# The openings of two feed-forward blocks: a tile in another ring, one split later, and another order ahead of the fourth token tile

## The chip, the cores and the metric

The kernel runs on one core of one Trainium2 chip. The core has five engines that work side by side, each through a queue of its own in order: TensorE (PE, matrix products), VectorE (DVE), ScalarE (ACT), GpSimd (POOL) and SyncE (SP), which here issues the transfers (DMA). They wait for each other by semaphores. The metric is the device time of one execution in microseconds (us). Before the change it is 2113.74 us, the median of 3 runs (2113.13 to 2113.86).

## The reference

One layer of a decoder trunk for 1024 tokens of width 1024, in float32: a feed-forward block, two attention branches with gates, and a second feed-forward block. Only the feed-forward blocks matter here:

```python
def rms_norm(x, gain):
    y = xf * lax.rsqrt(jnp.mean(xf * xf, axis=-1, keepdims=True) + RMS_EPS)
    return y * gain
def swiglu(x, w_gate, w_up, w_down):
    return (jax.nn.silu(x @ w_gate) * (x @ w_up)) @ w_down
...
x = x + 0.5 * swiglu(rms_norm(x, ffn1_norm), ffn1_w_gate, ffn1_w_up, ffn1_w_down)
x = x + mixer(x)
x = x + 0.5 * swiglu(rms_norm(x, ffn2_norm), ffn2_w_gate, ffn2_w_up, ffn2_w_down)
```

The hidden width is 2816, which is 22 tiles of 128.

## The kernel before

**Numbers.** Each float32 operand of a product is split into two float16 parts, a high one (a cast on ACT) and a low one (the remainder, on DVE); a product is then three matmuls (`mm3`): high by high, high by low, low by high. `part` runs one of these three for a whole tile and calls them H (weight high, tokens high), M (weight high, tokens low) and L (weight low, tokens high). Weights are first scaled by a power of two that comes from a bound on their size: `plain` holds the steps for a weight pair that is used as it is, `sums` (absolute sums, ACT), `spread` (two small matmuls into `mx`, a reduction and some one-column steps on DVE), `hi` (ACT) and `lo` (DVE).

**The opening of FFN 1** (`start`). The 1024 tokens lie in 8 token tiles of 128. `norm_steps` gives each tile six steps by letter: q square and row sum (ACT) and the reciprocal root (one step on ACT, three on POOL for tiles 1 to 7), s the product with root and gain into a buffer `y` of the ring (DVE), t eight transposes into a bank pair `psa` (PE), h high part (ACT), r a raw copy for the tiles 4 to 7 (ACT), l low part (DVE). `go` runs such steps in the order of its arguments. The first pair of weight tiles (gate and up, `p0`) is multiplied with tokens 0 to 511 (tiles 0 to 3) while tiles 4 to 7 are being prepared: H for gate and up, then M, M, L, L with a token tile's transposes between them.

**The rest of the opening** (`ffn_up`). The other half of the tokens for pair 0 (its result `a0` is written to DRAM), then pair 1 (`p1`) in full through `proj_T` (products `p2` and `p3`, result `a`). Pairs 2 to 21 are done in `hidden_tile` with seven products of sums in place of eight (Strassen's scheme): steps 0 to 6, each of 12 matmuls with an operand `op` made of weights (`split`, a cast on ACT at L164 and a low part on DVE at L165) and one made of tokens (`token_sums`: `total`, `high`, `low` for the four sums t1 to t4). Step 6 of a tile is put behind step 0 of the next one (`finish`). Step 6 reuses the bank `a` after DVE's L922 has read it. For tile 2 the sum t4 (`total(4)`, `high(4)`, `low(4)`) is made during the tile, through the list `mid`: it is the token operand of step 6.

**Rings.** `self.ring.tile` with a tag takes one of `bufs` buffers (two for each tag here); the next user of a buffer waits until its last use is over, and a transfer to DRAM counts as a use. The ring `y` holds the `y` of the token tiles, both halves `a0` of pair 0, `a` of pair 1 and the `sums` of the weight pairs (POOL). The ring `atp` holds the gain, the two halves of t3 and every fourth `op`; the other ops go to `stg`, `whi`, `wlo`.

**Order.** Inside `with self.in_order(...)` ACT, DVE and PE keep the order of the code; elsewhere (tiles 3 to 21, POOL, SP) a scheduler sets the order. FFN 2 runs the same `ffn_up`, but its tiles 4 to 7 are prepared in `first_half`.

Of the kernel before, what the change touches and what calls it, by code (L numbers as in the profile page):

```python
# [9 lines left out]
F32 = mybir.dt.float32  # L10
F32R = mybir.dt.float32r
BF16 = mybir.dt.bfloat16
F16 = mybir.dt.float16
I32 = mybir.dt.int32
AF = mybir.ActivationFunctionType
ALU = mybir.AluOpType
AX = mybir.AxisListType

P = 128
# [3 lines left out]
KD = D // P  # L23
# [13 lines left out]
HALF = 512  # L37
# [27 lines left out]
class Layer:  # L65
# [132 lines left out]
    def plain(self, loads, norm, engine=None):  # L198

        nc = self.nc  # L200
        st = self.sm.tile([P, 6], F32, tag="bst", bufs=2, name="bst")
        flat = lambda w: w.rearrange("p k n -> p (k n)")
        box = {}

        def sums():
            last = self.latest(mybir.EngineType.Activation)
            for k, w in enumerate(loads):
                nc.scalar.activation(
                    self.spare[:, :512].bitcast(BF16), flat(w), AF.Abs, accum_out=st[:, k:k + 1]
                )  # L210
                self.follow(last)

        def biggest():
            for k, w in enumerate(loads):
                nc.vector.tensor_reduce(
                    out=st[:, k:k + 1], in_=flat(w), op=ALU.max, axis=AX.X, apply_absolute_value=True
                )

        def spread():
            m = st[:, 5:6]  # L220
            self.spread_max(st, len(loads), m)
            box["s"], box["inv"] = self.pow2(m, 14, st[:, 2:5], norm["inv"])

        def hi():
            h, l = (self.ring.tile([P, 2, KD, P], F16, tag=t, bufs=2, name=t) for t in ("whi", "wlo"))
            box["w"] = [(h[:, a], l[:, a]) for a in range(2)]
            for (o, _), w in zip(box["w"], loads):
                nc.scalar.activation(o, w, AF.Copy, scale=box["s"])

        def lo():  # L230
            for (h, o), w in zip(box["w"], loads):
                nc.vector.scalar_tensor_tensor(
                    out=flat(o), in0=flat(w), scalar=box["s"], in1=flat(h), op0=ALU.mult, op1=ALU.subtract
                )

        box.update(sums=sums, biggest=biggest, spread=spread, hi=hi, lo=lo)
        return box

# [95 lines left out]
    def start(self, norm, loads, small, row, tags):  # L334
        ET = mybir.EngineType
        nc = self.nc
        steps = lambda t: self.norm_steps(norm, t, nc.gpsimd if t else None)
        with self.in_order(ET.Activation, ET.DVE, ET.PE):
# [21 lines left out]
            n = {t: steps(t) for t in range(4)}  # L360
            p0 = self.plain([l[0] for l in loads], norm, nc.gpsimd)
            go = lambda *a: [n[int(b[1])][b[0]]() for b in a]
# [1 line left out]
            self.scale_gain(norm)  # L364
            go("t0", "q1", "h0", "s1", "t1", "q2", "l0", "q3", "h1", "s2", "t2")
            p0["sums"]()
            go("l1", "s3", "t3", "h2")
            p0["spread"]()
            n.update({t: steps(t) for t in range(4, NT)})
            ahead = {j: self.pair_load("ffn1", j, tags["w"]) for j in (2, 3)}  # L370
            go("l2", "h3")
            p0["hi"]()
            go("q4", "l3")
            banks = pg, pu = self.psbg(), self.psbg()
            (wg, wu), (hi, lo) = p0["w"], (norm[k][0] for k in ("hi", "lo"))
            self.part(pg, wg, hi, lo, "H")
            self.part(pu, wu, hi, lo, "H")
            p0["lo"]()
            p1 = self.plain([l[0] for l in self.ffn_loads("ffn1", 1)], norm, nc.gpsimd)
            go("q5", "s4", "t4")  # L380
            self.part(pg, wg, hi, lo, "M")
            go("h4", "r4", "s5", "t5", "l4", "q6")
            self.part(pu, wu, hi, lo, "M")
            go("h5", "r5", "s6", "l5", "q7", "t6")
            self.part(pg, wg, hi, lo, "L")
            go("s7", "h6", "r6", "l6", "t7")
            self.part(pu, wu, hi, lo, "L")
            go("h7", "r7", "l7")
            self.mark()
# [268 lines left out]
    def ffn_up(self, norm, name, p0, p1, banks, tags, loads, ready):  # L658
# [5 lines left out]
        nc = self.nc  # L664
# [3 lines left out]
        total, high, low, every = self.token_sums(norm)  # L668
# [6 lines left out]

        def out(n, pg, pu):
            s = slice(n * HALF, (n + 1) * HALF)
            a = self.ring.tile([P, HALF], F32, tag="y", bufs=2, name="a0")
            nc.scalar.activation(a, pg, AF.Silu, scale=p0["inv"])
            nc.vector.scalar_tensor_tensor(out=a, in0=pu, scalar=p0["inv"], in1=a, op0=ALU.mult, op1=ALU.mult)  # L680
            nc.sync.dma_start(dst[0][:, s], a)

        with self.in_order(ET.Activation, ET.DVE, ET.PE):
# [33 lines left out]
            ops = [next(nxt) for _ in range(2)]  # L717
# [3 lines left out]
            a = self.ring.tile([P, T], F32, tag="y", bufs=2, name="a")  # L721
# [4 lines left out]
            nc.vector.scalar_tensor_tensor(out=a, in0=p3, scalar=p1["inv"], in1=a, op0=ALU.mult, op1=ALU.mult)  # L726
            nc.sync.dma_start(dst[1], a)
            tile = self.up_tiles(norm, name, tags, loads, stats, scales, sumd)
            ops, finish = tile(2, ops, every, None, (lambda: total(4), lambda: (high(4), low(4))))
        for j in range(3, NH):  # L730
            ops, finish = tile(j, ops, every, finish, ())
        finish()
# [148 lines left out]
    def hidden_tile(self, ops, tok, e, nxt, finish, then, inv, late, mid):  # L881


        nc = self.nc
# [8 lines left out]
        def prep():  # L893
            new.extend(o for o in (next(nxt, None),) if o is not None)
# [21 lines left out]
        step(4, c, False)  # L916
        v(out=e[:, 1], in0=c, in1=e[:, 1], op=ALU.add)
        nc.scalar.activation(e[:, 1], e[:, 1], AF.Silu, scale=inv)
        prep()
        step(5, a, False)  # L920
        stt = nc.vector.scalar_tensor_tensor
# [942 lines left out]
```

## Time and profile before

| what | before |
|---|---|
| median of 3 runs | 2113.74 us |
| the profiled execution | 2112.18 us |
| its span (first to last instruction) | 2110.4 us |
| mean granted TensorE clock | 0.994 |
| PE / DVE / ACT / POOL busy | 98% / 63% / 50% / 33% |

The times in the views are microseconds from the start of the span. The duration of a row of matmuls is modelled and overlaps the next one a little. "Granted clock" is the share of its full clock at which PE was allowed to run. In names, an arrow points from what is read to what is written: `psa<-ident,y` are transposes of a `y` into `psa`. A group `x8` is eight like instructions in one row.

### The profile page before, as it was taken

What the parts mean: (1) busy time and instruction counts of PE and PEld (TensorE: products, weight loads), DVE (VectorE), ACT (ScalarE), POOL (GpSimd) and SP (SyncE); (2) the same over time, 40 slices, a digit from 0 to 9 for tenths busy, and PEclk for the clock granted to TensorE, in tenths of its full rate; (3) what the DMA queues carried; (4) which work ended last, traced back from release to release, by engine and by line L of the source; (5) the groups of instructions that cost most, each with busy time, mean ns of one, the idle gap of its engine ahead of it and who ended that gap; (6) DMA issues with size and microseconds to landing.
All of it is one profiled execution on the core that took longest, in us unless ns stands there. A gap on an engine that the chain in (4) does not pass through costs nothing.

```text
span 2110.4 us, 28351 instructions
## 1 busy us (share of the span) xinstructions
PE 2077.0 (98%) x10199; PEld 1436.4 (68%) x10199; DVE 1330.4 (63%) x2317; ACT 1054.6 (50%) x1845; POOL 697.1 (33%) x741
## 2 busy tenths in 40 slices
PE   7999999999999999999999999999999999999999
PEld 4444444458888888888888888888444444448887
DVE  6755555577776787455656677864754545559765
ACT  7555555534444554356656775422555555544442
POOL 2355554572301112123333432000244555465200
PEclk8999999999999999999999999999999999999999
DMA  7134243464424387664556683641443433355432
GB/s 205 55 101 149 87 139 100 140 255 158 131 91 161 109 229 203 219 168 138 142 140 153 183 221 114 219 140 66 107 128 100 139 100 119 121 190 214 135 101 109
DMA packets 251638, 304.87 MB, mean 144 GB/s; under 512 B 17785, under 2 KB 186601, under 8 KB 251498
## 3 DMA queue, kind: packets, MB, share of 16 engines
q1 hardware_dynamic: 251498, 303.07, 47.2%
q8 instruction: 80, 1.31, 0.3%
q14 instruction: 60, 0.49, 0.1%
HBM read 205.02 MB, written 98.00 MB: 144 GB/s over the span
## 4 chain that ended last, share of the span: by engine, by line
PE 86%; DVE 5%; ACT 3%; DMA 3%; issue 2%; POOL 1%; SPq 0%; ACTq 0%; POOLq 0%; DVEq 0%
PE pst L876 18%; PE psd L1026 17%; PE psb L876 10%; PE pss L1647 4%; PE psg L876 3%; PE pspt L1673 3%; PE psgate L154 3%; PE psgate L155 3%; PE psgate L156 3%; PE pspv L1684 3%; PE psb L156 2%; PE psb L154 2%; PE psb L155 2%; PE psin L154 1%; PE psin L156 1%
## 5 line engine op out<-in xcount | busy, mean ns | idle before, releaser
L876 PEld LDWEIGHTS <-op 128*128 128x128 f16 x3360 | 329.5, 98 | 400.1 <-issue 7.0
L1026 PE MATMUL psd<-op 128*128 128x512 f32 x1680 | 383.9, 390 | 2.0 <-DVE op L162 2.0
L1026 PEld LDWEIGHTS psd<-op 128*128 128x128 f32 x1680 | 314.9, 188 | 69.8 <-DVE op L162 4.1
L876 PE MATMUL pst<-s_u,op 128*128 128x512 f16 x720 | 167.8, 383 | 4.2 <-DVE s_act L922 4.2
L876 PE MATMUL pst<-s_v,op 128*128 128x512 f16 x720 | 166.7, 382 | 2.9 <-DVE s_u L922 2.9
L1654 ACT ACTIVATE s_act<-pss,nm 128x128 f32<-128x128 f32 (+7 forms) x128 | 95.0, 743 | 97.6 <-DVE nm L1651 97.3
L161 ACT CAST op<-s_u 128x512 fp32r<-128x512 f32 x120 | 74.4, 620 | 107.8 <-PE psd L1026 91.0
L162 DVE TENSOR_TENSOR op<-s_u,op 128x512 fp32r<-128x512 f32 x120 | 103.6, 863 | 37.2 <-ACT op L161 37.1
L165 DVE SCALAR_TENSOR_TENSOR op<-s_act,s_wd,op 128x512 f16<-128x512 f32 x100 | 82.9, 844 | 56.2 <-ACT op L164 56.1
L165 DVE SCALAR_TENSOR_TENSOR op<-s_u,s_v,op 128x512 f16<-128x512 f32 x100 | 82.1, 837 | 56.5 <-ACT op L164 56.5
L1647 PE MATMUL pss<-s_wd 96*128 96x256 f32 (+5 forms) x480 | 112.7, 361 | 0.0
L161 ACT CAST op<-s_wd 128x512 fp32r<-128x512 f32 x95 | 59.0, 621 | 106.1 <-PE psd L1026 98.2
L851 POOL TENSOR_TENSOR sums<-s_u 128x512 f32<-128x512 f32 x20 | 25.9, 1293 | 258.1 <-PE psa L586 158.0
L1692 DVE TENSOR_TENSOR cmb<-pspv,cmb 64x512 f32<-64x512 f32 x64 | 44.1, 688 | 103.6 <-ACT cmb L1691 103.2
L164 ACT ACTIVATE op<-s_u,s_v 128x512 f16<-128x512 f32 x100 | 68.3, 716 | 75.2 <-DVE s_v L178 69.8
L162 DVE TENSOR_TENSOR op<-s_wd,op 128x512 fp32r<-128x512 f32 x95 | 80.2, 844 | 36.7 <-ACT op L161 36.7
L164 ACT ACTIVATE op<-s_act,s_wd 128x512 f16<-128x512 f32 x100 | 68.2, 716 | 70.0 <-DVE s_wd L178 64.3
L154 PE MATMUL psgate<-s_u,whi 128*128 128x512 f32 x256 | 101.6, 397 | 0.1
L1677 DVE TENSOR_TENSOR s_v<-pspt,s_v 128x512 fp32r<-128x512 f32 (+1 forms) x160 | 96.3, 631 | 7.2 <-ACT s_v L1676 5.6
L155 PE MATMUL psgate<-s_u,whi 128*128 128x512 f32 x256 | 100.8, 394 | 0.0
L156 PE MATMUL psgate<-s_u,wlo 128*128 128x512 f32 x256 | 100.4, 392 | 0.0
L1651 DVE TENSOR_REDUCE nm<-pss 128x1 f32<-128x128 f32 (+7 forms) x128 | 93.5, 749 | 1.5
(528 smaller groups left out, 4642.7 us busy)
## 6 DMA issues: line engine op xcount, KB each, us to landing
sumd<-s_u SPq DMA_DIRECT2D x20, 1024.0 KB, 6.4
sumd<-s_wd SPq DMA_DIRECT2D x13, 1024.0 KB, 5.1
s_wd<-fd SPq DMA_DIRECT2D x48, 256.0 KB, 5.4
s_u<-in_ffn_w_down_dram SPq DMA_DIRECT2D x22, 512.0 KB, 5.7
s_wd<-sumd SPq DMA_DIRECT2D x14, 768.0 KB, 4.2
s_u<-sumd SPq DMA_DIRECT2D x14, 768.0 KB, 4.4
s_act<-in_ffn_w_gate_dram SPq DMA_DIRECT2D x20, 512.0 KB, 3.8
s_act<-in_ffn_w_up_dram SPq DMA_DIRECT2D x20, 512.0 KB, 5.3
```

Source lines behind the costliest of these rows:

```text
L154: mm(out, lhsT=lh, rhs=rh, start=start, stop=False)
L155: mm(out, lhsT=lh, rhs=rl, start=False, stop=False)
L156: mm(out, lhsT=ll, rhs=rh, start=False, stop=stop)
L161: self.nc.scalar.copy(hi, src)
L162: self.nc.vector.tensor_tensor(out=lo, in0=src, in1=hi, op=ALU.subtract)
L164: self.nc.scalar.activation(hi, src, AF.Copy, scale=scale)
L165: self.nc.vector.scalar_tensor_tensor(out=lo, in0=src, scalar=scale, in1=hi, op0=ALU.mult, op1=ALU.subtract)
L876: mm(out, lhsT=a[:, k, :], rhs=b[:, k, :], start=start and k == 0 and i == 0, stop=k == n - 1 and i == 2, skip_group_check=True,)
L1026: nc.tensor.matmul(o, lhsT=u[:, r], rhs=w, start=start and m == 0, stop=k == CK - 1 and m == 2, skip_group_check=True,)
L1647: mm(ps[:, b:e], lhsT=a[:, q], rhs=bb[:, b:e], start=k == 0, stop=k == len(passes) - 1)
L1654: nc.scalar.activation(pn[:, :n], ps[:, :n], AF.Exp, bias=nm, accum_out=rs[:, i, j:j + 1])
L1677: nc.vector.tensor_tensor(out=lo, in0=pt[:, s0:], in1=hi, op=ALU.subtract)
```

## The change

There are three edits. In `start` the squares of tiles 4 to 7 go together ahead of the second part's work, the spread of pair 0 goes ahead of the transposes of tile 3 (the fourth token tile), and `hi` and `lo` of pair 0 are called for gate and up one at a time, `lo` ahead of the H products. In `out` the second half's `a0` takes a buffer of `atp` in place of `y`. In `hidden_tile` `low(4)` is called on its own, behind the SiLU of step 4. The last two run in both FFNs. (The argument `nc.gpsimd` of `plain` was not used in it.)

```diff
@@ plain
-        def hi():
-            h, l = (self.ring.tile([P, 2, KD, P], F16, tag=t, bufs=2, name=t) for t in ("whi", "wlo"))
-            box["w"] = [(h[:, a], l[:, a]) for a in range(2)]
-            for (o, _), w in zip(box["w"], loads):
-                nc.scalar.activation(o, w, AF.Copy, scale=box["s"])
+        def hi(*which):
+            if "w" not in box:
+                h, l = (self.ring.tile([P, 2, KD, P], F16, tag=t, bufs=2, name=t) for t in ("whi", "wlo"))
+                box["w"] = [(h[:, a], l[:, a]) for a in range(2)]
+            for k in which or range(2):
+                nc.scalar.activation(box["w"][k][0], loads[k], AF.Copy, scale=box["s"])
...
@@ start
             p0["sums"]()
-            go("l1", "s3", "t3", "h2")
+            go("l1", "s3")
             p0["spread"]()
+            go("t3", "h2")
             n.update({t: steps(t) for t in range(4, NT)})
             ahead = {j: self.pair_load("ffn1", j, tags["w"]) for j in (2, 3)}
+            p0["hi"](0)
             go("l2", "h3")
-            p0["hi"]()
+            p0["lo"](0)
+            p0["hi"](1)
             go("q4", "l3")
+            p0["lo"](1)
             banks = pg, pu = self.psbg(), self.psbg()
             (wg, wu), (hi, lo) = p0["w"], (norm[k][0] for k in ("hi", "lo"))
             self.part(pg, wg, hi, lo, "H")
             self.part(pu, wu, hi, lo, "H")
-            p0["lo"]()
-            p1 = self.plain([l[0] for l in self.ffn_loads("ffn1", 1)], norm, nc.gpsimd)
-            go("q5", "s4", "t4")
+            p1 = self.plain([l[0] for l in self.ffn_loads("ffn1", 1)], norm)
+            go("q5", "s4", "q6", "t4", "s5", "q7")
             self.part(pg, wg, hi, lo, "M")
-            go("h4", "r4", "s5", "t5", "l4", "q6")
+            go("h4", "r4", "t5", "s6", "l4")
             self.part(pu, wu, hi, lo, "M")
-            go("h5", "r5", "s6", "l5", "q7", "t6")
+            go("h5", "r5", "t6", "s7", "l5")
             self.part(pg, wg, hi, lo, "L")
-            go("s7", "h6", "r6", "l6", "t7")
+            go("h6", "r6", "l6", "t7")
             self.part(pu, wu, hi, lo, "L")
@@ ffn_up, out
-            a = self.ring.tile([P, HALF], F32, tag="y", bufs=2, name="a0")
+            a = self.ring.tile([P, HALF], F32, tag="y" if n == 0 else "atp", bufs=2, name="a0")
@@ ffn_up
-            ops, finish = tile(2, ops, every, None, (lambda: total(4), lambda: (high(4), low(4))))
+            ops, finish = tile(2, ops, every, None, [lambda: total(4), lambda: high(4), lambda: low(4)])
@@ hidden_tile
         step(4, c, False)
         v(out=e[:, 1], in0=c, in1=e[:, 1], op=ALU.add)
         nc.scalar.activation(e[:, 1], e[:, 1], AF.Silu, scale=inv)
+        if mid:
+            mid[2]()
         prep()
         step(5, a, False)
```

Line numbers in the changed kernel are 2 to 7 higher behind these places (L722 becomes L727, L917 becomes L922, L922 becomes L929).

ACT in the opening of FFN 1, from the second absolute sum of pair 0 (L208) on. L594 is a token tile's high part, L228 the `hi` of pair 0, L571 with L118 a square, L601 a raw copy. Before:

```order
L208 ACTIVATE s_wd_147,bst_156<-stg_85 128x1024
L594 CAST s_u_154<-psa_230 128x4x128 x2
L594 CAST s_u_154<-psa_245 128x4x128 x2
L228 ACTIVATE whi_279<-stg_83,bst_156 128x1024
L228 ACTIVATE whi_279<-stg_85,bst_156 128x1024
L571 ACTIVATE s_wd_147,ss_283<-s_v_74 128x1024
L118 ACTIVATE r1y_286<-ss_283,eps_96 128x1
L571 ACTIVATE s_wd_147,ss_320<-s_v_74 128x1024
L118 ACTIVATE r1y_323<-ss_320,eps_96 128x1
L594 CAST s_u_265<-psa_332 128x4x128 x2
L601 COPY s_v_267<-psa_332 128x4x128
```

ACT at the same place in the changed kernel (L599 is the high part, L229 `hi`, L576 the square):

```order
L208 ACTIVATE s_wd_147,bst_156<-stg_85 128x1024
L599 CAST s_u_154<-psa_230 128x4x128 x2
L229 ACTIVATE whi_275<-stg_83,bst_156 128x1024
L599 CAST s_u_154<-psa_254 128x4x128 x2
L229 ACTIVATE whi_275<-stg_85,bst_156 128x1024
L576 ACTIVATE s_wd_147,ss_284<-s_v_74 128x1024
L118 ACTIVATE r1y_287<-ss_284,eps_96 128x1
L576 ACTIVATE s_wd_147,ss_320<-s_v_74 128x1024
L118 ACTIVATE r1y_323<-ss_320,eps_96 128x1
L576 ACTIVATE s_wd_147,ss_332<-s_v_75 128x1024
L118 ACTIVATE r1y_335<-ss_332,eps_96 128x1
L576 ACTIVATE s_wd_147,ss_353<-s_v_75 128x1024
```

The first half of `hi` moved ahead of tile 3's high part, and all four squares stand ahead of tile 4's high part, where two of them stood behind it.

ACT in FFN 1 around the result `a` of pair 1 (L722, L727), with the engines or transfers that each row waits for; `a0_612` is the second half of pair 0, DMAHW are transfers. Before:

```order
L679 ACTIVATE a0_612<-psg_461,bst_156 128x512 [waits DMAHW2_49,PE_49]
L793 CAST s_wd_489<-t3_534 128x4x256
L722 ACTIVATE a_618<-psa_541,bst_319 128x1024 [waits DMAHW3_49,DVE_49,PE_49]
L838 ACTIVATE s_wd_147<-s_act_272 128x2048 [waits DMAHW7_49,DMAHW6_49,Activation_49]
L164 ACTIVATE op_671<-s_act_269,s_wd_147 128x512 [waits Pool_49]
L164 ACTIVATE op_674<-sums_601,s_wd_147 128x512 [waits Pool_49]
```

ACT at the same place in the changed kernel:

```order
L684 ACTIVATE a0_612<-psg_461,bst_156 128x512 [waits PE_49]
L798 CAST s_wd_489<-t3_534 128x4x256
L727 ACTIVATE a_618<-psa_541,bst_319 128x1024 [waits DMAHW2_49,PE_49]
L843 ACTIVATE s_wd_147<-s_act_272 128x2048 [waits DMAHW7_49,DMAHW6_49,Activation_49]
L164 ACTIVATE op_671<-s_act_269,s_wd_147 128x512 [waits Pool_49]
L164 ACTIVATE op_674<-sums_601,s_wd_147 128x512 [waits DVE_49,Pool_49]
```

The order is the same. `a_618` waited for the write of `a0_612` (DMAHW3) and now waits for that of the first half (DMAHW2); `op_674` waits for DVE as well.

DVE at the end of tile 2 in FFN 1: L797 (L802) is `low(4)`, L917 (L922) adds step 4, L922 (L929) reads the bank for step 6. Before:

```order
L165 SCALAR_TENSOR_TENSOR op<-sums,s_wd,op 128x512
L797 TENSOR_TENSOR s_v<-s_v 128x2048
L917 TENSOR_TENSOR s_u<-psb,s_u 128x512
L165 SCALAR_TENSOR_TENSOR op<-s_act,s_wd,op 128x512 x2
L922 SCALAR_TENSOR_TENSOR s_u<-pst,s_wd,s_u 128x512
```

DVE at the same place in the changed kernel:

```order
L165 SCALAR_TENSOR_TENSOR op<-sums,s_wd,op 128x512
L922 TENSOR_TENSOR s_u<-psb,s_u 128x512
L802 TENSOR_TENSOR s_v<-s_v 128x2048
L165 SCALAR_TENSOR_TENSOR op<-s_act,s_wd,op 128x512
L929 SCALAR_TENSOR_TENSOR s_u<-pst,s_wd,s_u 128x512
```

`low(4)` moved behind the add, and one operand's low part moved behind L929. On PE at this place, in FFN 1 alone, the scheduler had put the first six matmuls of tile 3's step 1 ahead of step 6 of tile 2; in the changed kernel all twelve stand behind it. On SP the two loads of pair 1 stand one or two loads earlier. In the opening PE's order differs only by the spread's two matmuls, now ahead of tile 3's transposes.

More of the change, by code (lines that the diff above doesn't have):

```diff
@@ L222, in spread, with lo @@
             box["s"], box["inv"] = self.pow2(m, 14, st[:, 2:5], norm["inv"])
-        def hi():
-            h, l = (self.ring.tile([P, 2, KD, P], F16, tag=t, bufs=2, name=t) for t in ("whi", "wlo"))
-            box["w"] = [(h[:, a], l[:, a]) for a in range(2)]
-            for (o, _), w in zip(box["w"], loads):
-                nc.scalar.activation(o, w, AF.Copy, scale=box["s"])
-        def lo():
-            for (h, o), w in zip(box["w"], loads):
+        def hi(*which):
[4 more added lines that the diff above has]
+                nc.scalar.activation(box["w"][k][0], loads[k], AF.Copy, scale=box["s"])
+        def lo(*which):
+            for k in which or range(2):
+                h, o = box["w"][k]
                 nc.vector.scalar_tensor_tensor(
-                    out=flat(o), in0=flat(w), scalar=box["s"], in1=flat(h), op0=ALU.mult, op1=ALU.subtract
+                    out=flat(o), in0=flat(loads[k]), scalar=box["s"], in1=flat(h), op0=ALU.mult, op1=ALU.subtract
                 )
```

## The prediction

> **What bounds the kernel now.** I read the page's span and busy table first.
>
> ```profile
> span 2110.4 us, 28351 instructions
> ...
> PE 2077.0 (98%) x10199; PEld 1436.4 (68%) x10199; DVE 1330.4 (63%) x2317; ACT 1054.6 (50%) x1845; POOL 697.1 (33%) x741
> ```
>
> TensorE (PE) is busy 98% of the span. The change touches no matmul, so it can win only where PE stands still or runs at a low granted clock. The view of PE's waits says where it stands still; a row ends with the sum in us, the count and the longest wait.
>
> ```profile
> PE psa L586 <- DVE y L579: 8.0, 7, 2.0
> PE pst L876 <- DVE s_act L922: 4.2, 1, 4.2
> PE pst L876 <- DVE s_u L922: 2.9, 1, 2.9
> ...
> PE psb L876 <- ACT s_u L909: 1.1, 1, 1.1
> ...
> PE psg L876 <- ACT s_act L909: 0.6, 1, 0.6
> ```
>
> L586 is mostly the opening of FFN 1; the L876 rows are one place in each FFN, tile 2 of `hidden_tile`. Then the stretches at low clock. The view of windows, with PE's rows alone, gives each stretch's length, PE's busy time and, after the bracket, the granted clock:
>
> ```profile
> 12.58:26.24 13.66, 8.76 (x31) 0.50 1.14 333
> 33.07:36.48 3.41, 1.87 (x14) 1.00 0.93 211
> 94.50:97.91 3.41, 1.06 (x5) 1.00 0.10 27
> 97.91:101.33 3.42, 3.42 (x10) 0.50 1.04 280
> 1538.34:1541.75 3.41, 0.60 (x3) 1.00 0.14 38
> 1541.75:1548.58 6.83, 5.40 (x14) 0.50 1.13 288
> ```
>
> The clock is halved in three stretches of 13.66, 3.42 and 6.83 us: 4, 1 and 2 times 3.41. The second and third follow 3.41 us in which PE was busy for only 1.06 and 0.60 us; a stretch with 1.87 us busy, which holds a stall of 1.5 us, cost no clock. So a long stall is paid twice: work at half clock loses half its time, 3.42/2 = 1.7 us in FFN 1, 5.40/2 = 2.7 us in FFN 2.
>
> The Trainium skill ("TensorE: Matmul & The Clock Gate", section "What's actually happening") has the clock drop after an idle window of about 3.4 us and calls the window free-running. The trace agrees on the length, not on "idle": 1.06 us of work in the window did not save the clock, so the measurement decides. By the page alone the 2.9 us stall would cost no clock, and the sum below would be 1.7 us smaller.
>
> **Part A, the opening of FFN 1.** Rows of the timelines of ACT, PE, DVE and POOL: start, duration, engine, line, operation, and in brackets the idle time before; the last row is a window of all engines, and ends with the clock, the transfers' share and their GB/s.
>
> ```profile
> 16.55 0.19 ACT L208 ACTIVATION_READ_ACCUMULATOR s_wd<-stg 128x1 f32 x1
> ...
> 21.02 2.19 ACT L228 ACTIVATE whi<-stg,bst 128x1024 f16<-128x1024 f32 x2 [0.80 <-DVE bst L177]
> ...
> 40.12 1.07 ACT L594 CAST s_u<-psa 128x512 f16<-128x512 f32 x2
> ...
> 18.90 1.06 PE L191 MATMUL mx<-ident,bst 128*128 128x128 f32 x4
> 22.22 5.59 PE L400 MATMUL psb<-s_u,whi 128*128 128x512 f16 x16 [2.26 <-ACT whi L228]
> 28.12 1.07 PE L586 MATMUL psa<-ident,y 128*128 128x128 f32 x8 [0.31 <-DVE y L579]
> ...
> 35.06 1.06 PE L586 MATMUL psa<-ident,y 128*128 128x128 f32 x8 [1.54 <-DVE y L579]
> ...
> 38.45 1.06 PE L586 MATMUL psa<-ident,y 128*128 128x128 f32 x8 [0.59 <-DVE y L579]
> 39.35 1.89 PE L400 MATMUL psb<-s_u,wlo 128*128 128x512 f16 x8
> 41.08 1.89 PE L400 MATMUL psg<-s_u,whi 128*128 128x512 f16 x8
> ...
> 20.00 0.42 DVE L196 TENSOR_REDUCE bst<-mx 128x1 f32<-128x256 f32 x1 [2.98 <-PE mx L191]
> ...
> 26.74 1.29 POOL L117 TENSOR_SCALAR r1a<-ss 128x1 f32<-128x1 f32 x1
> ...
> 36.00:37.00 1.00, 1.00 (x7) 0.46 (x5) 0.11 (x1) 0.92 (x3) 0.61 (x2) 1.00 0.11 6
> ```
>
> The spread (`mx`) needs the two sums, which end at 16.55 + 0.19 = 16.74. Ahead of tile 3's transposes it runs at 16.8 to 17.8; from its reduction to the first `hi` took 21.02 - 20.00 = 1.0 us, so `hi(0)` starts at 18.85 and ends 1.1 us later (half of 2.19), at 20.0. Tile 3's transposes slip to about 17.8 to 19.7, its high half follows `hi(0)`, and the first H matmul can start after half of that, at 20.6 instead of 22.22. At half clock until 26.24 these 1.6 us are worth half: the H products end 0.8 us earlier, at 26.9.
>
> Then tiles 4, 6 and 7 kept PE waiting 0.31, 1.54 and 0.59 us. A row's modelled end lies 0.16 us behind the next start (39.35 + 1.89 against 41.08), so start to start it was 2.9 us. Their chain is square (ACT), three small steps (POOL), product `y` (DVE). In the new order ACT does four squares from 22.0 to 27.5, and DVE makes `y` of tile 4 by 26.2, before the H products end. I keep POOL's long form, 1.29 us for the first small step beside a DVE product: then the `y` end 2.2 us apart (28.4, 30.6), each before PE gets there (29.5, 32.1), and tile 7's, behind tile 4's low half on DVE, at 33.2 against 34.7. All three waits go.
>
> PE reaches the second half (41.08 before) at 37.35, 3.7 us earlier. What is late next is tile 7's high half: it started 40.12 - 36.12 = 4.0 us behind tile 6's transposes (35.06 + 1.06), with tile 6's copies, a table load and a SiLU ahead of it on ACT. These transposes now end at 33.0, so half of it is there at 37.5, 0.15 us late. **A = 3.55 us.** Bounds: 2.5 if POOL's step collides once more, 4.3 if the clock comes back one window earlier. Pair 1's loads move past one or two others on SP's queue; all loads have landed by 36, where the traffic falls to 6 GB/s, and pair 1's sums come at 39, so that costs nothing; without this cover each us late costs one.
>
> **Part B, tile 2 of FFN 1.** The same kind of rows, of ACT, PE and DVE:
>
> ```profile
> 70.67 1.11 ACT L722 ACTIVATE a<-psa,bst 128x1024 f32<-128x1024 f32 x1 [4.10 <-DMA actd<-a]
> ...
> 75.41 0.71 ACT L164 ACTIVATE op<-sums,s_wd 128x512 f16<-128x512 f32 x1
> ...
> 72.82 2.75 PE L876 MATMUL pst<-s_u,op 128*128 128x512 f16 x12
> 75.41 0.38 PE L191 MATMUL mx<-ident,s_wd 128*128 128x128 f32 x2
> ...
> 68.43 1.91 DVE L797 TENSOR_TENSOR s_wd<-t,s_wd 128x1024 f16<-128x1024 f32 x1
> ...
> 77.63 1.28 DVE L726 SCALAR_TENSOR_TENSOR a<-psa,bst,a 128x1024 f32<-128x1024 f32 x1
> ...
> 91.10 2.28 DVE L797 TENSOR_TENSOR s_v<-s_v 128x2048 f16<-128x2048 f32 x1
> 93.30 0.68 DVE L917 TENSOR_TENSOR s_u<-psb,s_u 128x512 f32<-128x512 f32 x1
> ...
> 95.38 0.75 DVE L165 SCALAR_TENSOR_TENSOR op<-s_act,s_wd,op 128x512 f16<-128x512 f32 x1 [0.74 <-ACT op L164]
> 96.05 0.75 DVE L922 SCALAR_TENSOR_TENSOR s_u<-pst,s_wd,s_u 128x512 f32<-128x512 f32 x1
> ```
>
> ACT stood 4.10 us at L722 until the write of `a0` had left the ring `y`; behind it stood a statistic and five operand casts, and DVE waited for those. With `a0` in `atp` that wait goes. What is late next: the fourth and fifth of these casts (75.41 is the fourth) go into slots that the matmuls of `p3` read, so they cannot start before `p3` ends, at 72.82 by the row of the next matmuls. From there two casts (0.7 us each) and a DVE operand put L726 about 2.05 us behind `p3`'s end, where it was 77.63 - 72.82 = 4.81: **2.76 us won on DVE's chain.** The ring `atp` adds two waits. The second of the five casts waits for the low half of the last t3 (L797, which ended at 70.34 and now ends about 0.1 us after that cast's turn; behind it on ACT stand casts that wait for `p3` anyway). The first cast of pair 3 waits for `a0`'s write, over by some 6 us before its turn. I take 0 for both; one cast, 0.7 us, is the other bound.
>
> From L726 to L922 it took 96.05 - 77.63 = 18.42 us. Now the low half of the last token sum (2.28 us) stands behind L917, so the SiLU and the cast for which DVE waited from 93.98 to 95.38 run beside it: **1.4 us shorter, 17.0.** L922 then ends 2.05 + 17.0 + 0.75 = 19.8 us after `p3`. Until there PE has seven products of 2.59 us (75.41 - 72.82) and an `mx` of 0.2, 18.35 us in all. So step 6 waits 1.5 us, and the 1.1 us wait in step 4 goes, since L909 moves up by more than that.
>
> Before, PE lost here 1.1 + 2.9, with 0.16 on each 4.3 start to start, and 1.7 of clock: 6.0 us. After: 1.5, and with 1.9 us busy in any window of 3.41 the clock holds as in the row with 1.87. Six matmuls (1.3 us) that stood ahead of step 6 now stand behind it; they are the same work, so the sum of waits already has them. **B = 4.5 us**, bounds 2.0 (clock lost and the chain 0.8 longer) and 5.5.
>
> **Part C, tile 2 of FFN 2.**
>
> ```profile
> 1517.00 1.12 ACT L722 ACTIVATE a<-psa,bst 128x1024 f32<-128x1024 f32 x1 [3.76 <-DMA actd<-a]
> ...
> 1519.67 2.75 PE L876 MATMUL pst<-s_act,op 128*128 128x512 f16 x12
> ...
> 1523.96 1.28 DVE L726 SCALAR_TENSOR_TENSOR a<-psa,bst,a 128x1024 f32<-128x1024 f32 x1
> ...
> 1542.38 0.74 DVE L922 SCALAR_TENSOR_TENSOR s_act<-pst,s_v,s_act 128x512 f32<-128x512 f32 x1
> ```
>
> The same figures: L726 came 4.29 us after `p3`'s end (1519.67) and 18.42 before L922. With 2.05 and 17.0 the stall shrinks to 1.5 us. Before, it lost 0.6 + 4.2, start to start 5.1, and 2.7 of clock: 7.8 us. **C = 6.3 us**, bounds 3.0 and 7.0. The opening of FFN 2 has another code path, so part A has no counterpart here.
>
> **The sum.** 3.55 + 4.5 + 6.3 = 14.35 us. The profiled execution took 2112.18 us, 1.8 of it around the span; less 14.35 is 2097.8. The median shown, 2113.74, is 1.56 above it, so I forecast 2099.4. Behind both places PE has no wait over 1.5 us, and the later stages are set off by PE's own progress, so nothing should give the time back.
>
> **Rivals.** (1) *The clock still drops.* If L922 comes 0.7 us later than worked out, the gap is 2.2 us, and PE is busy for 1.2 us of an unlucky window, close to the 1.06 that lost it. Price: 0.7 + 1.7 in FFN 1, 0.7 + 2.7 in FFN 2; in both 5.8 us: 2105.2. For it: one more DVE and POOL collision is enough, as the 1.29 us row shows; against it: the collisions of the old chain are already in the 18.42. Chance 0.17. (2) *The wait only changes its name:* the slots in `atp` hold ACT as long as the transfer did, and only A and the reordered low halves are left, 3.55 + 1.4 + 1.4: 2107.4. Against it: their releases come 2 us or more ahead of `p3`'s end. Chance 0.05. (3) *Hidden anyway:* something behind FFN 1 is timed by transfers, and 11 us or more come back: 2111. PE's waits show no sign of it: 0.04. (4) *Slower:* the six matmuls behind step 6. If an ACT wait that I do not see keeps L922 where it was, PE has nothing to fill the gap: 1.3 us, 2.6 at half clock. It decides as soon as A is gone too, if the spread, now ahead of tile 3's transposes in PE's queue, waits for a late weight load and holds all behind it, us for us; 4 us late gives 2113.7 + 2.6 + 4 = 2120.3. Against it: the sums ended at 16.74, before tile 3's `y`. Chance 0.02.
>
> **How the numbers follow.** Forecast 0.72 at 2099.4, its own range 2097 to 2102.5. With rival 1 and the early clock of part A the range is 2096.5 to 2106.0; rivals 2 to 4 lie outside it. A measurement of this kernel tells 0.2%, 4.2 us, from no change. Faster by that: 0.72 + 0.17 + 0.05, less 0.02 for mixed mishaps, 0.92; within 0.06; slower 0.02.
>
> **What would show it.** L722's successor follows the t3 cast on ACT with no wait for a transfer; L726's stands 2 us behind `p3`'s end; in both FFNs step 6 waits 1.2 to 1.8 us and the granted clock stays 1.00 behind it; the mean clock rises from 0.994 to 0.997; the first H matmul is at 20.6, no tile from 4 to 7 makes PE wait, and the second half starts near 37.5. A stall over 2 us in either tile 2, or a slow stretch there, would prove the chain mis-sized.

## The result, and the profile after

The changed kernel takes 2099.77 us, the median of 4 runs (2097.71 to 2101.86); the kernel before, timed beside it, 2113.43 us (2112.17 to 2113.86). The ratio is 0.9930, with a 95% interval of 0.9916 to 0.9945. The forecast was 2099.4 us.

The page of the changed kernel, its head and its first line of engines:

```profile
span 2095.9 us, 28351 instructions
...
PE 2071.5 (99%) x10199; PEld 1435.6 (68%) x10199; DVE 1332.3 (64%) x2317; ACT 1055.9 (50%) x1845; POOL 702.2 (34%) x741
```

The span fell by 14.5 us. PE's busy time fell by 5.5 us, though it does the same matmuls: that part is the clock (mean 0.998 in place of 0.994). PE's waits in the changed kernel (sum, count, longest):

```profile
PE pst L881 <- DVE s_u L929: 1.3, 1, 1.3
PE pst L881 <- DVE s_act L929: 1.3, 1, 1.3
```

The two L881 rows were 2.9 and 4.2 us, and the waits in step 4 are gone. Windows of PE's rows: the stretch at half clock in the opening with the window ahead of it, and the window in FFN 1 that holds step 6's wait (length, PE busy, granted clock behind the bracket):

```profile
5.09:8.51 3.42, 3.42 (x16) 1.00 0.89 327
8.51:18.75 10.24, 7.19 (x31) 0.50 1.09 357
87.02:90.43 3.41, 2.13 (x11) 1.00 0.00 0
```

The opening's stretch is the only one at half clock; those at 98 and 1542 us are gone. Tile 2 of FFN 1 and of FFN 2 on PE: the matmuls that start at the end of `p3`, those that wait at step 6, and the first into `psb` behind them.

```profile
69.25 2.75 PE L881 MATMUL pst<-s_u,op 128*128 128x512 f16 x12
...
89.04 2.76 PE L881 MATMUL pst<-s_v,op 128*128 128x512 f16 x12 [1.28 <-DVE s_u L929]
...
94.45 2.75 PE L881 MATMUL psb<-s_wd,op 128*128 128x512 f16 x12
...
1511.57 2.75 PE L881 MATMUL pst<-s_act,op 128*128 128x512 f16 x12
...
1531.35 2.76 PE L881 MATMUL pst<-s_u,op 128*128 128x512 f16 x12 [1.27 <-DVE s_act L929]
...
1534.17 2.75 PE L881 MATMUL psb<-s_act,op 128*128 128x512 f16 x12
```

From the first to the last of these: 25.20 us in FFN 1 and 22.60 in FFN 2. In the kernel before `p3` ended at 72.82 and 1519.67 us, and the first matmuls into `psb` behind step 6 are these:

```profile
102.65 2.75 PE L876 MATMUL psb<-s_wd,op 128*128 128x512 f16 x12
...
1548.64 2.75 PE L876 MATMUL psb<-s_act,op 128*128 128x512 f16 x12
```

That is 29.83 and 28.97 us. On ACT and DVE the cause shows: L727 no longer waits for a transfer, L731 stands 2.08 us behind `p3`'s end (4.81 before), and L929 16.92 us behind L731 (18.42 before), with `low(4)` (L802) where DVE had been idle for 1.4 us.

```profile
62.79 1.11 ACT L727 ACTIVATE a<-psa,bst 128x1024 f32<-128x1024 f32 x1
...
71.33 1.28 DVE L731 SCALAR_TENSOR_TENSOR a<-psa,bst,a 128x1024 f32<-128x1024 f32 x1
...
85.39 2.28 DVE L802 TENSOR_TENSOR s_v<-s_v 128x2048 f16<-128x2048 f32 x1
...
88.25 0.74 DVE L929 SCALAR_TENSOR_TENSOR s_u<-pst,s_wd,s_u 128x512 f32<-128x512 f32 x1
```

The opening, on ACT, PE and DVE:

```profile
18.88 1.15 ACT L229 ACTIVATE whi<-stg,bst 128x1024 f16<-128x1024 f32 x1 [0.95 <-DVE bst L177]
...
14.70 1.94 PE L591 MATMUL psa<-ident,y 128*128 128x128 f32 x8 [1.07 <-DVE y L584]
...
20.55 3.61 PE L405 MATMUL psb<-s_u,whi 128*128 128x512 f16 x16 [1.34 <-ACT s_u L599]
26.26 1.06 PE L591 MATMUL psa<-ident,y 128*128 128x128 f32 x8 [2.10 <-DVE y L584]
...
31.82 1.07 PE L591 MATMUL psa<-ident,y 128*128 128x128 f32 x8 [0.17 <-DVE s_u L612]
...
37.51 0.81 PE L405 MATMUL psg<-s_u,whi 128*128 128x512 f16 x3 [0.30 <-ACT s_u L599]
...
24.83 1.28 DVE L584 SCALAR_TENSOR_TENSOR y<-s_v,r1r,gain 128x1024 f32<-128x1024 f32 x1 [0.90 <-POOL r1r L120]
```

The second half starts at 37.51 in place of 41.08. Tile 2's transposes start at 14.70 here; before they started at 14.47:

```profile
14.47 1.94 PE L586 MATMUL psa<-ident,y 128*128 128x128 f32 x8 [1.88 <-DVE y L579]
```

The wait of tile 7 is gone and that of tile 6 down to 0.17, but tile 4 waits 2.10 us where it waited 0.31: the clock came back at 18.75 instead of 26.23, the H products were done at 24.0, and tile 4's `y` came at 24.83 + 1.28 = 26.11.

The three places give 41.08 - 37.51 = 3.57, 29.83 - 25.20 = 4.63 and 28.97 - 22.60 = 6.37 us, 14.57 in all, against 14.5 by the spans: nothing was given back between them or behind them.

### The profile page after: what moved, and what is told of

Same layout as the page of the kernel before. It is cut to its first block, busy times and chain, and to the rows that moved or that the text cites. A ratio compares the mean times of both kernels' runs of the same rounds, so it can differ in the third digit from the quotient of the medians.

```text
span 2095.9 us, 28351 instructions
## 1 busy us (share of the span) xinstructions
PE 2071.5 (99%) x10199; PEld 1435.6 (68%) x10199; DVE 1332.3 (64%) x2317; ACT 1055.9 (50%) x1845; POOL 702.2 (34%) x741
## 4 chain that ended last, share of the span: by engine, by line
PE 89%; DVE 4%; DMA 2%; ACT 2%; POOL 1%; issue 1%; SPq 0%; ACTq 0%; POOLq 0%; DVEq 0%
PE pst L881 18%; PE psd L1033 17%; PE psb L881 10%; PE pss L1654 4%; PE psg L881 3%; PE pspt L1680 3%; PE psgate L154 3%; PE psgate L155 3%; PE psgate L156 3%; PE pspv L1691 3%; PE psb L156 2%; PE psb L155 2%; PE psb L154 2%; PE psin L154 2%; PE psin L156 2%; PE psin L155 2%
## 5 line engine op out<-in xcount | busy, mean ns | idle before, releaser
L881 PEld LDWEIGHTS <-op 128*128 128x128 f16 x3360 | 328.5, 98 | 391.1 <-DVE s_u L929 1.8
L881 PE MATMUL pst<-s_v,op 128*128 128x512 f16 x720 | 165.2, 379 | 1.3 <-DVE s_u L929 1.3
L881 PE MATMUL pst<-s_u,op 128*128 128x512 f16 x720 | 165.2, 379 | 1.3 <-DVE s_act L929 1.3
L856 POOL TENSOR_TENSOR sums<-s_u 128x512 f32<-128x512 f32 x20 | 25.8, 1292 | 255.2 <-PE psa L591 158.0
```

Of the source, the lines that this page charges most:

```text
L881: mm(out, lhsT=a[:, k, :], rhs=b[:, k, :], start=start and k == 0 and i == 0, stop=k == n - 1 and i == 2, skip_group_check=True,)
```

## The experiments

**Each edit alone, and the changed kernel again.** The theory is the prediction's sum: three places, the clock among their prices. Its rivals are that one edit does nearly all, or that the edits share one wait, so that each alone already has most of it.

The opening alone is the changed kernel with the ring and the order of `low(4)` put back:

```diff
-            a = self.ring.tile([P, HALF], F32, tag="y" if n == 0 else "atp", bufs=2, name="a0")
+            a = self.ring.tile([P, HALF], F32, tag="y", bufs=2, name="a0")
...
-            ops, finish = tile(2, ops, every, None, [lambda: total(4), lambda: high(4), lambda: low(4)])
+            ops, finish = tile(2, ops, every, None, (lambda: total(4), lambda: (high(4), low(4))))
...
-        if mid:
-            mid[2]()
```

> The opening's edit alone (ring and low(4) as before). My theory: the second half of the opening starts 3.5 us earlier than before (near 37.5), p3 ends 3.5 us earlier, and nothing in tile 2 changes: the ACT wait for the transfer of some 4 us, the step 4 wait of 1.1 and the step 6 waits of 2.9 and 4.2 us all stand; the time falls by 3.5 us, by 1.7 more if the window's phase spares the clock in FFN 1. Rival (opening hidden): p3 ends where it did and the time stays within 1 us of before.

The ring alone, on the kernel before:

```diff
-            a = self.ring.tile([P, HALF], F32, tag="y", bufs=2, name="a0")
+            a = self.ring.tile([P, HALF], F32, tag="y" if n == 0 else "atp", bufs=2, name="a0")
```

> The ring edit alone. My theory: in both FFNs L726 starts 2.05 us behind p3's end (4.81 and 4.29 before) and L922 still 18.42 behind L726; step 4 of tile 2 waits for nothing; step 6 waits about 2.0 us in FFN 1 (four matmuls of the next tile now stand ahead of it) and 2.8 in FFN 2; the opening ends at 41.1 as before. Gain 4 to 4.6 us in FFN 1 and 2.3 to 5.0 in FFN 2, by whether the clock still drops. Rival (the wait only changes its name): ACT waits at the second of the five casts instead, L726 stays more than 4 us behind p3's end, gain under 1 us.

The later `low(4)` alone, on the kernel before:

```diff
-            ops, finish = tile(2, ops, every, None, (lambda: total(4), lambda: (high(4), low(4))))
+            ops, finish = tile(2, ops, every, None, [lambda: total(4), lambda: high(4), lambda: low(4)])
...
+        if mid:
+            mid[2]()
         prep()
         step(5, a, False)
```

> The late low(4) alone. My theory: the transfer still holds ACT for 4 us; L726 to the bank's read (L922 before, two lines further here) falls from 18.42 to 17.0 in both FFNs; in FFN 1 that is worth almost nothing (1.4 less 1.3 for the six matmuls that no longer fill the gap), in FFN 2 1.4 us; the clock still drops in FFN 2. Gain 1.5 us, up to 4 if the clock is kept in one place. Rival (the low half was the whole wait): step 6 waits under 1 us and the gain is 4 or more from each FFN.

All three, the changed kernel itself:

> The changed kernel once more, for the spread of its times (2097.7 to 2101.9, 4.2 us, where before had 1.7). If the phase of the clock's window makes it, the stretches at low clock differ between the two profiles by what the spans differ, and every wait of PE is the same to 0.2 us. If transfers make it, some wait behind FFN 1 differs by 2 us or more at an equal clock. Step 6 waits 1.3 us (modelled) in both FFNs again.

| kernel | median, us | ratio to before, 95% | tile 2, FFN 1 | tile 2, FFN 2 | opening |
|---|---|---|---|---|---|
| before | 2113.69 | | 29.83 | 28.97 | 26.61 |
| opening alone | 2109.63 | 0.9982 (0.9973 to 0.9992) | 29.33 | 28.79 | 22.79 |
| ring alone | 2108.91 | 0.9977 (0.9967 to 0.9986) | 25.82 | 25.77 | 26.59 |
| `low(4)` alone | 2111.13 | 0.9985 (0.9976 to 0.9994) | 29.61 | 26.55 | 26.92 |
| all three | 2102.99 | 0.9949 (0.9934 to 0.9964) | 25.21 | 22.59 | 22.79 |

Tile 2 is the time from `p3`'s end to the first `psb` matmul behind step 6, in the profile; the opening is the time from the start of tile 2's transposes to the second half (the profile before: 41.08 - 14.47). Each edit works at its own place (the opening alone also takes 0.5 us off tile 2 of FFN 1, where step 4's wait is shorter), and all three count: by the medians 4.06, 4.78 and 2.56 us, each with an interval of 2 us to either side, 11.4 in sum, and 10.7 together. But the two in tile 2 do not simply add up: the gains of the places are 4.0 + 3.2 us (ring) and 0.2 + 2.4 us (`low(4)`), 9.8 in sum, and 11.0 with both. PE's waits with the ring alone, then with `low(4)` alone:

```profile
PE pst L876 <- DVE s_act L922: 2.8, 1, 2.8
PE pst L876 <- DVE s_u L922: 1.9, 1, 1.9
```

```profile
PE pst L876 <- DVE s_act L924: 2.8, 1, 2.8
PE pst L876 <- DVE s_u L924: 2.7, 1, 2.7
```

The windows around these waits, ring alone and then `low(4)` alone:

```profile
94.94:98.35 3.41, 1.51 (x8) 1.00 0.14 37
...
1538.78:1542.19 3.41, 0.70 (x4) 1.00 0.87 245
1542.19:1545.60 3.41, 3.41 (x10) 0.50 1.22 290
```

```profile
93.30:96.72 3.42, 0.69 (x4) 1.00 0.00 0
96.72:100.13 3.41, 3.41 (x10) 0.50 0.09 25
```

A wait of 1.9 us left 1.51 us of work in its window, and the clock stayed; waits of 2.7 and 2.8 us left about 0.7, and the next window ran at half clock. Either edit alone leaves at least one stall that loses the clock; together they leave 1.3 us in both FFNs, and none does. In FFN 2 this is why the two win 0.8 us more together: before, the clock was low for two windows (6.83 us), each edit alone saves one (the other is 1542.19 to 1545.60 with the ring, 1543.98 to 1547.39 with `low(4)`), and only both save all. In FFN 1 the 0.4 us have another cause. The scheduler puts matmuls of the next tile ahead of step 6, where they fill part of the wait: six before, four with the ring alone, none with `low(4)` alone or with both. So `low(4)` alone moves the bank's read 1.5 us closer to `p3`'s end, but its stall shrinks only from 2.94 to 2.73 us and still costs a slow window (with the 1.1 us wait in step 4 still there): 0.2 us won. Each of these readings is from one profile; a stall of 2.7 us that falls on the border of two windows would leave more work in each, and no run here shows that case.

**What is left in tile 2.** In the sum for B and C step 6 still waits 1.5 us because DVE makes an operand ahead of L929. If so, two operands put behind L929 take the wait away:

```diff
@@ hidden_tile, tile 2 (mid) alone: two of the calls that make an operand move
         step(3, a, False)
         nc.scalar.copy(e[:, 1], a)
         if mid:
             mid[1]()
-        prep()
+        else:
+            prep()
...
         if mid:
             mid[2]()
-        prep()
+        else:
+            prep()
...
         nc.gpsimd.tensor_tensor(out=e[:, 1], in0=e[:, 1], in1=e[:, 2], op=ALU.mult)
+        if mid:
+            prep()
+            prep()
         prep()
```

> The changed kernel, and in tile 2 of both FFNs the two operands that DVE makes ahead of L929 (the second halves of the casts behind steps 3 and 4) are made behind it. If the 1.28 and 1.27 us that step 6 still waits come from DVE's own work ahead of L929, as the sum for B and C had it (operands of 0.75 us each stand there), L929 moves up by 1.3 us or more and step 6 waits 0 to 0.3 us: p3's end to the first matmul behind step 6 falls from 25.2 to 23.9 us in FFN 1 and from 22.6 to 21.3 us in FFN 2, and the kernel is 2.5 to 2.9 us faster than the changed kernel. The rival: L929 is held by ACT or by PE's own results, or the two operands come too late for the matmuls that use them, and the wait turns up there: 25.2 and 22.6 us stay, or the loss shows within 10 us behind step 6.

The changed kernel beside it:

> The changed kernel itself once more, beside the others of this call on one chip. Its two medians so far were 2099.8 and 2103.0 us, its ratios to the kernel before 0.9934 and 0.9949 by the medians. If its time differs by the clock at the start of each execution, and not by the chip, its runs spread over 3 us or more here as well, and its profile shows the same 25.2 and 22.6 us in tile 2 and 22.8 us in the opening.

Both once more, timed side by side again:

> The kernel with the operands behind L929 once more, beside the changed kernel on one chip: 2.5 to 2.9 us less than the changed kernel's median if the waits of step 6 (1.45 us start to start in each FFN) were all there was; if only the draw of the clock at the start made the difference of the last call, within 1 us of it.

> The changed kernel itself, the measure for the others of this call: 25.2 and 22.6 us in tile 2 of the two FFNs and 22.8 us in the opening whatever the total, 2097.5 to 2103.7 us as in its runs so far, and no stretch at half clock behind the opening.

| comparison | changed kernel | operands behind L929 |
|---|---|---|
| first | 2100.78 (2098.96 to 2103.37), ratio 0.9940 (0.9928 to 0.9953) | 2098.11 (2096.76 to 2099.57), ratio 0.9927 (0.9914 to 0.9941) |
| second | 2101.60 (2099.43 to 2104.39), ratio 0.9935 (0.9923 to 0.9948) | 2098.25 (2096.43 to 2099.24), ratio 0.9917 (0.9904 to 0.9931) |

Five runs each, ratios to the kernel before (2113.0 and 2115.6 us). The changed kernel's own runs spread over 4.4 and 5.0 us, with 22.8 us in the opening in both profiles; one of them, 2104.39, is above the 2103.7 us that were expected at most. The medians differ by 2.7 and 3.4 us. The intervals overlap; what settles it is the timeline of PE and DVE in FFN 1 with the operands behind L929:

```profile
69.29 2.75 PE L881 MATMUL pst<-s_u,op 128*128 128x512 f16 x12
...
87.64 2.75 PE L881 MATMUL pst<-s_v,op 128*128 128x512 f16 x12
...
93.04 2.75 PE L881 MATMUL psb<-s_wd,op 128*128 128x512 f16 x12
...
86.43 0.74 DVE L931 SCALAR_TENSOR_TENSOR s_u<-pst,s_wd,s_u 128x512 f32<-128x512 f32 x1
87.09 0.74 DVE L165 SCALAR_TENSOR_TENSOR op<-sums,s_wd,op 128x512 f16<-128x512 f32 x1
```

The bank's read moved from 88.25 to 86.43, step 6 waits for nothing, and `p3`'s end to the `psb` matmul is 23.75 us instead of 25.20; in FFN 2 it is 21.16 instead of 22.60. That is 2.9 us, as expected, and the operands are still made in time. It is the fastest form of tile 2 found.

**The opening's two edits apart.** The earlier spread alone puts the order of tiles 4 to 7 back; the squares alone puts the spread, `hi` and `lo` back. Both keep the new tile 2.

```diff
@@ the earlier spread alone
-            go("q5", "s4", "q6", "t4", "s5", "q7")
+            go("q5", "s4", "t4")
             self.part(pg, wg, hi, lo, "M")
-            go("h4", "r4", "t5", "s6", "l4")
+            go("h4", "r4", "s5", "t5", "l4", "q6")
             self.part(pu, wu, hi, lo, "M")
-            go("h5", "r5", "t6", "s7", "l5")
+            go("h5", "r5", "s6", "l5", "q7", "t6")
             self.part(pg, wg, hi, lo, "L")
-            go("h6", "r6", "l6", "t7")
+            go("s7", "h6", "r6", "l6", "t7")
@@ the squares alone
-            go("l1", "s3")
-            p0["spread"]()
-            go("t3", "h2")
+            go("l1", "s3", "t3", "h2")
+            p0["spread"]()
...
-            p0["hi"](0)
             go("l2", "h3")
-            p0["lo"](0)
-            p0["hi"](1)
+            p0["hi"]()
             go("q4", "l3")
-            p0["lo"](1)
...
             self.part(pu, wu, hi, lo, "H")
+            p0["lo"]()
```

> The changed kernel with the squares, scales and products of tiles 4 to 7 in the order of before; the spread ahead of tile 3's transposes and the halves of pair 0's weights one by one stay. The time from the start of tile 2's transposes to FFN 1's second half was 26.6 us before and is 22.8 in the changed kernel. If the two edits add up as in part A, this keeps the 0.8 to 1.5 us of the earlier H products and loses the waits of tiles 6 and 7 (1.54 and 0.59 us): 25.1 to 25.8 us. The rival: the chain of the squares sets tiles 5 to 7 whatever H does, and the earlier spread buys nothing by itself: 26.6 us.

> The changed kernel with the spread behind tile 3's transposes and the halves of pair 0's weights made together, as before; the new order of the squares, scales and products of tiles 4 to 7 stays. The time from the start of tile 2's transposes to FFN 1's second half was 26.6 us before, is 22.8 in the changed kernel and was 24.5 with the earlier spread alone. If the two edits add up, this one takes away 1.7 us alone: 24.9 us, with no wait for tiles 6 and 7 and the first H product 7.7 us behind tile 2's transposes, as before (22.22 - 14.47). The rival: the earlier spread only made room that the squares fill, and this edit alone gives less than 1 us: 25.6 us or more.

PE's timeline with the earlier spread alone, from tile 2's transposes to the second half:

```profile
14.64 1.94 PE L591 MATMUL psa<-ident,y 128*128 128x128 f32 x8 [1.35 <-DVE y L584]
...
33.12 1.07 PE L591 MATMUL psa<-ident,y 128*128 128x128 f32 x8 [1.53 <-DVE y L584]
...
36.52 1.06 PE L591 MATMUL psa<-ident,y 128*128 128x128 f32 x8 [0.60 <-DVE y L584]
...
39.14 1.02 PE L405 MATMUL psg<-s_u,whi 128*128 128x512 f16 x4
```

39.14 - 14.64 = 24.5 us: 2.1 of the 3.8 us are the spread's, with the waits of tiles 6 and 7 as before. With the squares alone:

```profile
17.45 1.94 PE L588 MATMUL psa<-ident,y 128*128 128x128 f32 x8 [3.45 <-DVE y L581]
...
42.34 1.89 PE L402 MATMUL psg<-s_u,whi 128*128 128x512 f16 x8 [0.30 <-ACT s_u L596]
```

42.34 - 17.45 = 24.9 us, 1.7 less than before, with no wait over 0.3 us behind tile 4. 2.1 + 1.7 = 3.8: the edits add up, and both rivals fall (nothing from the spread alone, less than 1 us from the squares alone). The spread gave more than expected, 24.5 us against 25.1 to 25.8. Each of the two kernels ran once (2100.24 and 2103.92 us), so only the places are compared here.

**Tile 4's square first.** With the operands behind L929 as base, to see whether tile 4's `y` sets the opening's end:

```diff
             p0["lo"](0)
-            p0["hi"](1)
-            go("q4", "l3")
+            go("q4")
+            p0["hi"](1)
+            go("l3", "q5", "s4")
             p0["lo"](1)
...
-            go("q5", "s4", "q6", "t4", "s5", "q7")
+            go("q6", "t4", "s5", "q7")
```

> The kernel of the first experiment of the last call (operands behind L929), and in the opening the square of tile 4 ahead of the second half of pair 0's high weights on ACT, its product y ahead of their low half on DVE. Theory: with the clock back early, tile 4's y sets the end of the opening (the 2.10 us wait); it then starts 1.1 us earlier, PE waits 0.9 us for the second high half instead, and 21.7 us lie between the start of tile 2's transposes and the second half instead of 22.8: 1 us less where that wait was 2.1 us, 0 to 0.3 us more where the clock came back late and the wait was 0.3 us. Rival: H products or ACT's copies set the end, and 22.8 us stay or grow. Tile 2 of both FFNs as in that kernel: no wait at step 6.

2097.76 us (2095.49 to 2101.05), ratio 0.9920 (0.9907 to 0.9933), beside 2098.25 for its base: no difference that these runs can tell. PE's timeline:

```profile
14.59 1.94 PE L592 MATMUL psa<-ident,y 128*128 128x128 f32 x8 [1.20 <-DVE y L585]
...
31.34 1.06 PE L592 MATMUL psa<-ident,y 128*128 128x128 f32 x8 [0.58 <-DVE s_u L613]
...
37.03 1.89 PE L406 MATMUL psg<-s_u,whi 128*128 128x512 f16 x8 [0.29 <-ACT s_u L600]
```

Tile 4's wait of 2.10 us is gone and PE waits 1.02 us for the second high half, as expected, but 22.4 us lie between tile 2's transposes and the second half, only 0.4 less. Tile 5's square starts where it did (23.20 us on ACT, 23.30 in the changed kernel), so the later tiles come 0.5 us earlier and not 1.1, and tile 6 waits 0.58 us for DVE. So tile 4's chain does count, with a third of the gain expected.

**One-row matmuls and the clock.** In the profile of the changed kernel PE was busy in all of the window from 5.09 to 8.51, and yet the next one ran at half clock. In it lie four matmuls with one row (`gb`, which copy the norm's gain to all partitions). This kernel gives them 128 rows, 127 of them zeros:

```diff
-        row = head[0:1, :D + 16]
-        self.nc.sync.dma_start(row[:, :D], self.i["ffn1_norm"][0:1, :])
+        row = head[:, :D + 16]
+        self.nc.gpsimd.memset(row[:P - 1, :D], 0.0)
+        self.nc.sync.dma_start(row[P - 1:, :D], self.i["ffn1_norm"][0:1, :])
...
-                    g, lhsT=one.broadcast_to([1, P]), rhs=row[:, k * 512:(k + 1) * 512], start=True, stop=True
+                    g, lhsT=one.broadcast_to([P, P]), rhs=row[:, k * 512:(k + 1) * 512], start=True, stop=True
```

> The changed kernel; the four matmuls that spread the norm's gain over 128 partitions multiply 128 rows (127 of zeros) instead of one. In the changed kernel's profile PE's rows were busy almost without a gap from 5.3 to 8.5 us, half of it these matmuls, and yet the clock fell at 8.51 and stayed at half to 18.75; in another profile of it the same four matmuls took 3.8 instead of 2.0 us. Theory: one-row matmuls do not count as work for the clock. Then with 128 rows the window they lie in keeps or brings the full clock, no stretch at half clock begins between 7 and 13 us, and the runs lie within 2 us of each other and up to 3 us below the changed kernel's median. Rival: the clock at the start is set by the phase of the window and by the gap before tile 0's product alone: stretches and times as in the changed kernel, within 1 us.

2099.64 us (2098.29 to 2101.96), beside 2100.78 for the changed kernel: the runs spread over 3.7 us, not 2, and the median is 1.1 lower, within the spread. Its windows:

```profile
5.89:9.30 3.41, 3.22 (x17) 1.00 0.99 379
9.30:12.72 3.42, 1.38 (x11) 1.00 1.17 313
```

The window with the four matmuls kept the clock here, but the next one, with 1.38 us of work, lost it at 12.72 us, so a stretch at half clock began where the theory had none. The kernel before, with its one-row matmuls (5.51 to 7.59 us), shows the same pair of windows:

```profile
5.75:9.16 3.41, 3.41 (x17) 1.00 0.96 370
9.16:12.58 3.42, 1.38 (x11) 1.00 1.19 314
```

It kept the clock behind a window with one-row matmuls as well. So this run does not tell the theory from its rival: what lost the clock at 8.51 us stays open, and the 128 rows bring no time that can be measured.

## Why the prediction was right

**A, the opening: 3.55 foretold, 3.57 measured, and by another route.** The spread ran ahead of tile 3, `hi(0)` began at 18.88 (18.85 foretold), the first H matmul at 20.55 (20.6), tile 4's `y` ended at 26.11 (26.2), the second half began at 37.51 (37.5). The step that failed is "at half clock until 26.24 these 1.6 us are worth half: the H products end 0.8 us earlier, at 26.9", and with it "all three waits go" and the bound of 4.3 for an earlier clock. It left the stretch at half clock where the profile before had it. Here the clock came back at 18.75, H ended at 24.0, and PE then waited 2.10 us for tile 4. But an earlier clock did not give more: the opening took 22.8 us in every profile with both edits, whether the clock came back at 18.75 or, as in the changed kernel's repeat, at 27.35.

What sets tile 4 is its own chain, the square (ACT), POOL's steps and `y` (DVE). The prediction had it right to 0.1 us and took it to be covered by PE. Tile 4's square and POOL's second step before:

```profile
23.11 1.04 ACT L571 ACTIVATE s_wd<-s_v 128x1024 bf16<-128x1024 f32 x1
...
25.03 1.26 POOL L119 TENSOR_SCALAR r1t<-r1y,r1a 128x1 f32<-128x1 f32 x1
```

and in the changed kernel:

```profile
21.93 1.05 ACT L576 ACTIVATE s_wd<-s_v 128x1024 bf16<-128x1024 f32 x1
...
24.08 0.34 POOL L119 TENSOR_SCALAR r1t<-r1y,r1a 128x1 f32<-128x1 f32 x1
```

Counted from tile 2's transposes the square starts 1.41 us earlier, and from there to the start of `y` it takes 2.90 us in place of 3.58, with the shorter step on POOL. Together that is the 2.1 us which the earlier spread gave by itself.

So the terms were mis-sized in opposite ways. Up to tile 4's transposes 1.2 us were foretold (28.12 to 26.9) and 1.86 came (26.26); behind them 2.35 were foretold and 1.71 came, since of the 2.45 us of waits at tiles 6 and 7, start to start, 0.33 came back at tile 6 and 0.46 at the second half, where 0.15 had been booked. That the sum is right to 0.02 us is luck. The 3.57 also holds 0.23 us lost ahead of tile 2's transposes, which start at other times in other executions; from there on the place gave 3.8.

**B and C, tile 2: 4.5 and 6.3 foretold, 4.63 and 6.37 measured.** Step by step: L731 behind `p3`'s end 2.08 us (2.05 foretold), from there to L929 16.92 (17.0), step 6's stall 1.28 + 0.16 = 1.44 (1.5), no slow window behind it. The two single edits show the two steps apart: with the ring alone 2.07 and 18.41 us, with `low(4)` alone 4.81 and 16.91. The two added waits for `atp` cost nothing that shows.

**The rivals.** (1) The clock did not drop: a stall of 1.44 us leaves at least 1.97 us of work in a window of 3.41, and 1.51 was enough. The single edits show how near it was: each still has a stall of 2.7 us or more that loses the clock. (2) ACT did not wait in the other ring: the second of the five casts starts at 66.42 us, where the first ends. (3) Nothing came back: 14.57 at the three places, 14.5 in the span. (4) The six matmuls behind step 6 cost nothing; L929 moved, and that was its condition.

**The total.** 14.35 foretold against 14.5 in the profiles. The medians of four comparisons differ by 13.7, 10.7, 12.2 and 14.0 us, all less, and the changed kernel's own medians run from 2099.8 to 2103.0: that the first of them lay within 0.4 us of the forecast is luck too. The profiled run of the changed kernel was the fastest of its four. The first repeat's profile has a span 4.9 us longer with the same 25.2, 22.6 and 22.8 us at the three places. 3.16 of it is there before tile 2's transposes; part of the rest is in waits of 0.62, 0.41 and 0.23 us at 694, 769 and 1384 us, which come and go between executions.

## What to carry to other kernels

Price a stall with the clock that it costs, and look at edits for one stall together: two edits, each of which alone left a stall that lost the clock, were worth 9.8 us apart and 11.0 us together. In an opening find the chain that paces each step before converting time on PE at half clock: here the chain through ACT, POOL and DVE set the end, and an earlier clock on PE brought nothing. When a wait is left, look for work of no urgency ahead of the instruction that ends it; moving two operands gave another 2.9 us.

## What the runs showed of the hardware

**How much work keeps the clock.** Of the windows of 3.41 us at full clock, those with 0.59 to 1.38 us of busy PE lost the clock in the next window, those with 1.46 us or more kept it, but for six (0.59 is from the opening alone, 89.86 to 93.28 us, 1.46 from the ring alone, 23.26 to 26.67). The Trainium skill ("TensorE: Matmul & The Clock Gate", section "What's actually happening") names an idle window of about 3.4 us as the condition; the length agrees, but these windows were not idle, and the measurement decides. The six that do not fit are, like 5.09 to 8.51 in the changed kernel, from profiles with the short form of the one-row matmuls, described next: they hold these matmuls and 3.03 to 3.42 us of busy PE, and the next window ran at half clock. The like window of the kernel before kept it. Why is open.

**The first microseconds differ between executions of one kernel.** The four one-row matmuls, in the changed kernel's profile and in that of its last repeat:

```profile
5.28 1.98 PE L354 MATMUL gb<-s_wd 1*128 1x512 f32 x4
```

```profile
5.44 3.78 PE L354 MATMUL gb<-s_wd 1*128 1x512 f32 x4
```

They took 1.98 us in one and 3.78 in the other, nearly twice as long, and tile 2's transposes then start at 14.7 or at 17.4 us. That this is half clock is inferred from the durations: the view of windows gives a granted clock of 1.00 there (5.44 to 9.22 us). Of the thirteen profiles of this study with one-row matmuls seven have the short form, among them those of before and after, and six the long one. Of the changed kernel's four profiled runs the short one took 2097.71 us and the long ones 2100.78 to 2102.63, so this can be most of the spread of 3 to 5 us between runs of one kernel; the runs without a profile do not show their form. It is why single times here say little about an edit of 3 us, while the same places in two profiles of one kernel agree within 0.1 us.
